# Output projection with its sums and lo parts on VectorE, and a ConvFFN entry that runs three first products in a row with lo parts from adding transfers

## The chip, the core and the metric

The kernel runs on one core of a Trainium2 chip. Its engines work in parallel, each on its own queue in order: TensorE (PE), VectorE (DVE), ScalarE (ACT), GpSimd (POOL) and SyncE (SP), which here only issues transfers. The metric is the device time of one execution in microseconds, from the first to the last instruction with what lies around it; smaller is better.

## The reference

One decoder layer over 1024 positions of width 1024 in float32: three token mixers on the same normalised input, merged by sigmoid gates, one output projection to the residual stream, and a gated MLP with a causal convolution of width 3 (ConvFFN, inner width 2816). The part that the change touches:

```python
merged = (gates[:, :, 0] * (y_sb @ w_sb_out[l])
          + gates[:, :, 1] * (y_ml @ w_ml_out[l])
          + gates[:, :, 2] * (y_xa @ w_xa_out[l]))
x = x + merged @ w_o[l]

h = _rmsnorm(x, g_ffn[l])
u = _causal_dwconv(h @ w_up[l], ff_conv_w[l], ff_conv_b[l])
u_val, u_gate = jnp.split(u, 2, axis=-1)
x = x + (jax.nn.silu(u_gate) * u_val) @ w_down[l]
```

## The kernel before

**Products.** A float32 operand is split into a hi part (a copy by ACT, rounded to the format that PE takes) and a lo part (operand minus hi, by VectorE), by `split` (L128). A product of two split operands is three matmuls of 128x128 by 128x512 (`mm3`, L142 to L144: hi by hi, hi by lo, lo by hi). Large products are cut into 2x2 blocks and done with seven block products instead of eight, from sums and differences of blocks (Strassen-Winograd). `au`, `al`, `bu`, `bl` are the blocks of the moving operand, `t1` to `t4` their sums; `a1`, `b1`, `a2`, `b2` are the blocks of a weight, `s1`, `s2` and the differences their sums. Tiles come from pools by tag, each with a fixed number of buffers that are given out in turn; a new tile waits until its buffer's last user is done. The stages that matter follow each other so:

**Branch products** (L1117 on). Three branches `b` of eight iterations. Each iteration makes one block of 128 output channels for both halves of the positions: for each half 12 matmuls into one of two banks `ps_pj`, and VectorE evicts it with the gate (L1137 for the first branch; L1139, then the addition L1140, for the others). Every other iteration loads a weight `raw` that is split into `whi` and `wlo`, two buffers each. Gates come from DRAM into five `U` buffers. Beside the iterations of branches 1 and 2 runs `beside`, the generators `wo_sums(0)` and `wo_sums(1)`: they load eight pages of the output projection's weights (tag `pg`, L1071, into pages that branch 0 has given back), make four sums for each half on POOL, and for each sum call `spill` (L1076): ACT copies the hi part to a `y` tile, POOL subtracts it into another `y` tile (two buffers in all), and POOL stores this lo part to `slo_d` in DRAM.

**Output projection** (stages 1 to 7, `stage`, 48 matmuls each). Stages 1, 2 and 5 take weights as loaded; 3, 4, 6 and 7 take the sums by `sum_w` (L1173): ACT copies hi again, POOL loads lo from `slo_d`. In stage 7 VectorE also scales the upper half's four `full` pages by the row factors and splits them into `dau` and `dbu`, the operands `au` and `bu` of the ConvFFN.

**ConvFFN entry.** Each of 22 units is a generator `seven`, advanced by `next`; a unit's products are, in order, first (`a1` by `au`), second (`b1` by `bu`), t2 and t3, t1, and `bl` and t4. A weight half is split by `qring` into a pair of tiles from a ring of four (`whi` and `wlo`, two buffers each). The lower half's row factors are not known at the start: `rstd` sums the squares over the partitions on PE (L158), VectorE scales the sums, POOL takes the root (L150), `spread` makes a diagonal on VectorE (L166) and spreads it over the partitions on PE. Then VectorE makes `diff`, `full` and from them t2, t3, t1, `bl` and t4, in this order, with their splits. In the program order the first unit's first product stands ahead of `rstd`, its second between `rstd` and `spread`, and the first and second products of the next two units behind.

Instructions are listed in program order, and a list scheduler may pull them forward; `tc.high_priority(offset=n)` moves the instructions in it n places ahead.

Of the kernel before, what the change touches and what calls it, by code (L numbers as in the profile page):

```python
# [10 lines left out]
F32 = mybir.dt.float32  # L11
# [7 lines left out]
P = 128  # L19
D = 1024  # L20
S = 1024
# [21 lines left out]
def tile_hybrid_layer(ctx: ExitStack, tc: tile.TileContext, xT, memT, vecs, w_t, w_n, w_kv, w_if,  # L43
# [55 lines left out]
    def dtile(shape, name):  # L99
        return dr.tile(shape, F32, tag=name, name=name)  # L100
# [22 lines left out]
        return vec[:, i:i + n]  # L123


    SOON = 40

    def split(src, hi, lo, eng=None):  # L128
        nc.scalar.activation(hi, src, AF.Copy)  # L129
# [531 lines left out]

    def qring(src, soon=SOON):
        t = pair(turn(0, ("whi", "wlo")))
        with tc.high_priority(offset=soon):
            split(src, *t)
        return t

    def prod(p, a, b, start=True):
        for k in range(4):
            mm3(p, a[0][:, ts(k)], a[1][:, ts(k)], *b[k], start and k == 0, k == 3, not start)  # L670
# [16 lines left out]
        nc.vector.tensor_sub(a2, a1, a2)  # L687
        nc.vector.tensor_sub(s2, s1, a1)

    def seven(w1, w2, x, done, ready=None):  # L690

        w, s1, s2, hl1 = ready or ((*halves(w1, next(RAWS[0])), *halves(w2, next(RAWS[1]))), None, None, None)
        a1, b1, a2, b2 = w
        L, p2 = bank(turn(2, LONG)), bank(turn(3, SHORT))
        prod(L, hl1 or qring(a1), x["au"])
        c1 = wide()
        up, lo = c1[:, hs(1)], c1[:, hs(0)]
        nc.scalar.activation(up, L, AF.Copy)
        if ready:
            yield  # L700
        prod(p2, qring(b1), x["bu"])
        nc.vector.tensor_add(up, up, p2)
        if not ready:
            s1, s2 = half(), a1
            sums(w, s1, s2)
        yield
        prod(L, qring(s2, 1000 if ready else SOON), x["t2"], False)
        c2 = wide()
        nc.scalar.activation(c2[:, hs(1)], L, AF.Copy)
        R = bank(turn(3, SHORT))  # L710
        prod(R, qring(a2, 1000 if ready else SOON), x["t3"])
        yield
        prod(L, qring(s1), x["t1"], False)
        nc.scalar.activation(c2[:, hs(0)], L, AF.Copy)
        nc.vector.tensor_add(c2[:, hs(0)], c2[:, hs(0)], R)
        nc.vector.tensor_sub(b1, b1, s2)
        yield
        prod(L, qring(b1), x["bl"], False)
        nc.scalar.activation(lo, L, AF.Copy)
        done(0, c1)  # L720
        prod(R, qring(b2), x["t4"], False)
        nc.vector.tensor_add(c2[:, hs(1)], c2[:, hs(1)], R)  # L722
        done(1, c2)
        yield
# [326 lines left out]
    slo_d = dtile([4, 2, P, S], "slo_d")  # L1051

    def block(n, h):
        return merged[n // 4][h][n % 4 // 2][:, hs(n % 2)]
# [18 lines left out]

    ws = [[None, None] for _ in range(4)]

    def spill(i, j):  # L1076
        hi, lo = T([P, S], "y", F32R), T([P, S], "y")
        nc.scalar.activation(hi, ws[i][j], AF.Copy)
        nc.gpsimd.tensor_sub(lo, ws[i][j], hi.bitcast(F32))
        nc.gpsimd.dma_start(slo_d[i, j], lo)  # L1080

    def wo_sums(j):
        a1, a2 = wo_load(0, 0, j, "pg"), wo_load(0, 1, j, "pg")
        yield
        nc.gpsimd.tensor_sub(a2, a1, a2)
        ws[2][j] = a2
        spill(2, j)
        b2 = wo_load(1, 1, j, "pg")
        yield
        nc.gpsimd.tensor_sub(b2, b2, a2)  # L1090
        ws[1][j] = b2
        spill(1, j)
        b1 = wo_load(1, 0, j, "pg")
        yield
        nc.gpsimd.tensor_add(a1, a1, b2)
        ws[0][j] = a1
        spill(0, j)
        nc.gpsimd.tensor_sub(b1, b1, b2)
        ws[3][j] = b1
        spill(3, j)  # L1100
        yield

    def fine(src, *tags):
        t = [T([P, S], tag, F32R) for tag in (tags[0], tags[-1])]
# [11 lines left out]
    ths = {i: get_gate(i, "y") for i in range(2)}  # L1116
    ys = None  # L1117
    w1 = []
    beside = itertools.chain(wo_sums(0), wo_sums(1))
    for i in range(3 * KT):  # L1120
        b, n = i // KT, ORDER[i % KT]
        if n == 0:
# [48 lines left out]
        return wsplit(None, raw=wo_load(q, i, j, "raw"))  # L1171

    def sum_w(i, j):  # L1173
        t = [T([P, S], tag, F32R) for tag in ("whi", "wlo")]
        nc.scalar.activation(t[0], ws[i][j], AF.Copy)
        nc.gpsimd.dma_start(t[1], slo_d[i, j])
        return t

    def out_tiles(i, h, tag):
        t = [T([P, S], tag) for _ in range(2)]  # L1180
# [147 lines left out]
    def ffn_up(f):  # L1328
        ys = {}

        def done(g, c):
            i = g * NF + f
            ys[g] = y = T([P, S], "y")
            conv(c, [col(C_FW + 3 * i + 2 - s) for s in range(3)], col(C_FB + i), y)
            if g:
                nc.scalar.activation(y, y, AF.Silu)
                nc.vector.tensor_mul(ys[0], ys[0], y)
                if f // 2 == 5:
                    nc.sync.dma_start(act_d[5, f % 2], ys[0])
# [4 lines left out]
        return seven(w_up[f], w_up[NF + f], fx, done, early if f == 0 else None)  # L1344


    fd, fx = {}, {"au": bau, "bu": bbu}
# [276 lines left out]
```

## Time and profile before

| | us |
|---|---|
| median of three runs | 1661.03 |
| lowest and highest | 1660.67, 1663.19 |
| the profiled execution, its own time | 1663.59 |
| its span | 1661.8 |
| mean granted PE clock | 0.994 |

A row of the timeline gives start and duration in us, engine, line, operation, output and inputs, shape, count, and in brackets the idle time of the engine ahead of it with what ended it. A row of waits gives the waiting instruction, what it waited for, the total, the number of waits and the longest. DVE is VectorE, ACT ScalarE, POOL GpSimd, SPq SyncE's queue. Matmuls overlap, so their durations exceed the distance of their starts.

### The profile page before, as it was taken

Reading aid. Unit: us, or ns where it says so; the run is one execution under the profiler, and the core shown is the slowest. Engines: PE = TensorE matmul, PEld = TensorE weight load, DVE = VectorE, ACT = ScalarE, POOL = GpSimd, SP = SyncE. Lnnn points to the kernel's source line nnn. Section 1 sums busy time; section 2 is a strip of 40 time slices with the busy share of each in tenths; the row PEclk is TensorE's granted clock in tenths of the full one; section 3 lists DMA queues with packets and bytes.
Section 4 is the critical chain, followed back from the end, with each engine's and each line's share of the span. In section 5 each row is a group of like instructions: output and inputs, shape, how many; then the busy total and the mean of one; then the engine's idle time right before and its main releaser. Section 6 shows DMA issues by size and latency. Waiting matters only on the chain.

```text
span 1661.8 us, 21230 instructions
## 1 busy us (share of the span) xinstructions
PE 1621.1 (98%) x7959; PEld 1325.5 (80%) x7959; DVE 1227.1 (74%) x1669; ACT 837.7 (50%) x1278; POOL 144.4 (9%) x196
## 2 busy tenths in 40 slices
PE   8999999999999999999977999999999999999999
PEld 4878888888788888888766887788888888888887
DVE  5658888859665676766565878997778877789864
ACT  4557777546554445666311355555555544543431
POOL 1022222020000101000072000000000000000000
PEclk9999999999999999999989999999999999999999
DMA  8420011424325564336865344132222221487131
GB/s 295 153 65 27 32 39 64 161 88 149 124 96 170 184 190 158 122 127 203 284 234 199 121 157 151 57 114 89 76 77 76 89 101 52 170 311 241 40 135 72
DMA packets 102515, 220.05 MB, mean 132 GB/s; under 512 B 13384, under 2 KB 37256, under 8 KB 102412
## 3 DMA queue, kind: packets, MB, share of 16 engines
q1 hardware_dynamic: 100108, 210.30, 37.4%
q0 software_dynamic: 2304, 8.39, 1.6%
q8 instruction: 63, 1.03, 0.3%
q14 instruction: 40, 0.33, 0.1%
HBM read 159.86 MB, written 58.80 MB: 132 GB/s over the span
## 4 chain that ended last, share of the span: by engine, by line
PE 86%; DMA 5%; DVE 3%; issue 3%; POOL 2%; ACT 2%; SPq 0%; POOLq 0%; DVEq 0%; ACTq 0%
PE ps_pj L142 12%; PE ps_pj L143 12%; PE ps_pj L144 12%; PE ps_pv L142 5%; PE ps_pv L144 5%; PE ps_pv L143 5%; PE ps_tr L142 4%; PE ps_tr L144 4%; PE ps_tr L143 4%; PE ps_z L142 4%; PE ps_z L143 4%; PE ps_z L144 4%; PE ps_pv L440 2%; PE ps_tr L420 2%; DMA raw<-in_w_kv_dram 1%
## 5 line engine op out<-in xcount | busy, mean ns | idle before, releaser
L143 PE MATMUL ps_pj<-h,whi 128*128 128x512 f32 x520 | 205.5, 395 | 1.3 <-DVE h L130 1.3
L142 PE MATMUL ps_pj<-h,whi 128*128 128x512 f32 x440 | 178.2, 405 | 19.9 <-DVE U L1139 18.1
L129 ACT ACTIVATE whi<-raw 128x512 fp32r<-128x512 f32 (+1 forms) x101 | 82.5, 816 | 139.9 <-PE ps_pj L143 43.8
L144 PE MATMUL ps_pj<-h,wlo 128*128 128x512 f32 x352 | 139.5, 396 | 0.1
L831 DVE SCALAR_TENSOR_TENSOR y<-U,vec,y 128x1023 f32<-128x1023 f32 x88 | 112.6, 1280 | 8.2 <-ACT y L829 8.1
L143 PEld LDWEIGHTS ps_pj<-h,whi 128*128 128x128 f32 x520 | 99.3, 191 | 21.1 <-DVE h L130 1.6
L142 PEld LDWEIGHTS ps_pj<-h,whi 128*128 128x128 f32 x440 | 84.1, 191 | 38.3 <-DVE U L1139 19.4
L408 DVE TENSOR_TENSOR_SCAN U<-U 128x512 f32<-128x512 f32 (+3 forms) x96 | 92.9, 1009 | 21.9 <-POOL U L403 20.3
L142 PE MATMUL ps_pj<-pg,whi 128*128 128x512 f32 x268 | 105.2, 393 | 1.2 <-DVE pg L1137 1.2
L144 PE MATMUL ps_pj<-pg,wlo 128*128 128x512 f32 x248 | 96.8, 390 | 0.0
L130 DVE TENSOR_TENSOR wlo<-raw,whi 128x1024 fp32r<-128x1024 f32 x44 | 54.4, 1237 | 39.8 <-ACT whi L129 39.7
L144 PEld LDWEIGHTS ps_pj<-h,wlo 128*128 128x128 f32 x352 | 67.4, 192 | 15.2 <-DVE wlo L130 0.6
L143 PE MATMUL ps_pv<-h,whi 128*128 128x512 f32 x190 | 74.1, 390 | 0.0
L143 PE MATMUL ps_pj<-pg,whi 128*128 128x512 f32 x188 | 73.5, 391 | 0.0
L129 ACT ACTIVATE whi<-pg 128x512 fp32r<-128x512 f32 (+1 forms) x46 | 35.3, 768 | 62.7 <-PE ps_z L143 18.2
L829 ACT ACTIVATE y<-U,vec 128x1024 f32<-128x1024 f32 x44 | 54.6, 1241 | 17.2 <-DVE U L722 17.2
L144 PE MATMUL ps_pj<-h,whi 128*128 128x512 f32 x160 | 62.4, 390 | 0.0
L142 PEld LDWEIGHTS ps_pj<-pg,whi 128*128 128x128 f32 x268 | 50.4, 188 | 13.0 <-DVE pg L1137 2.7
L142 PE MATMUL ps_pv<-h,whi 128*128 128x512 f32 x150 | 59.0, 393 | 0.4 <-DVE U L722 0.4
L144 PE MATMUL ps_pv<-h,wlo 128*128 128x512 f32 x152 | 59.2, 390 | 0.0
L130 DVE TENSOR_TENSOR wlo<-raw,wlo 128x512 fp32r<-128x512 f32 x55 | 37.8, 688 | 26.2 <-ACT wlo L129 26.0
L397 ACT ACTIVATE U<-ps_z 128x1024 f32<-128x1024 f32 (+3 forms) x48 | 39.1, 814 | 31.9 <-PE ps_z L395 24.1
(484 smaller groups left out, 4543.5 us busy)
## 6 DMA issues: line engine op xcount, KB each, us to landing
raw<-in_w_t_dram SPq DMA_DIRECT2D x29, 512.0 KB
gate_d<-U SPq DMA_DIRECT2D x24, 512.0 KB
U<-gate_d SPq DMA_DIRECT2D x22, 512.0 KB
act_d<-y SPq DMA_DIRECT2D x22, 512.0 KB
pg<-in_w_t_dram SPq DMA_DIRECT2D x21, 512.0 KB
raw<-in_w_dn_dram SPq DMA_DIRECT2D x18, 512.0 KB
h<-act_d SPq DMA_DIRECT2D x14, 512.0 KB
raw<-in_w_br_dram SPq DMA_DIRECT2D x12, 512.0 KB
```

The costliest lines, as they stand in the source:

```text
L129: nc.scalar.activation(hi, src, AF.Copy)
L130: (eng or nc.vector).tensor_sub(lo, src, hi.bitcast(F32))
L142: nc.tensor.matmul(out, lh, rh, start=start, stop=False, skip_group_check=more)
L143: nc.tensor.matmul(out, lh, rl, start=False, stop=False, skip_group_check=more)
L144: return nc.tensor.matmul(out, ll, rh, start=False, stop=stop, skip_group_check=more)
L397: nc.scalar.activation(f[:, :, 1:w + 1], z[:, :, :w], AF.Sigmoid, scale=-0.125)
L408: nc.vector.tensor_tensor_scan(f[:, a, 1:w + 1], f[:, a, 1:w + 1], f[:, a, 1:w + 1], 1.0 if o == 0 else f[:, a, 0:1], op0=ALU.mult, op1=AL ...
L420: nc.tensor.transpose(pt[:, a, ts(j)], g[:, a, ts(j)], ident)
L440: nc.tensor.matmul(pv[64 * a:64 * a + 64, ts(rb % 4)], sbv[s // 2][:, s % 2, (2 * p + a) * 64:(2 * p + a + 1) * 64], wt[a][:, ts(j)], star ...
L829: nc.scalar.activation(out, u, AF.Identity, bias=bias, scale=taps[0])
L831: nc.vector.scalar_tensor_tensor(out[:, :S - s], u[:, s:], taps[s], out[:, :S - s], op0=ALU.mult, op1=ALU.add)
```

## The change

Four things change.

- `wo_sums` is one generator. It loads the eight pages over four iterations, and the eight sums are made in place by VectorE, one per iteration in program order. `spill` and the DRAM tensor `slo_d` are gone.
- `sum_w` splits a sum with `fine`: hi by ACT as before, lo by VectorE at the time of use. POOL has no part in the output projection's weights any more.
- `seven` gets `pause` (units 0 to 2): a break after the first product. The entry then runs the first products of units 0, 1 and 2, and behind them their second products; `rstd` stands behind the first of them and `spread` behind the second.
- `seven` gets `adds` (units 0 to 3): the lo parts of `a1`, `b1` and `b2`, which are weights as they stand in DRAM, are made by `qadd`: ACT copies hi, ACT copies minus hi into the lo tile, and a transfer by POOL adds the weight from DRAM to it (256 KB, 11 of them in all, since the first unit's `a1` keeps its early split). `LEAD` (60) takes the place of `SOON` (40) as their priority.

```diff
-    SOON = 40
+    SOON, LEAD = 40, 60
...
+    def qadd(src, dram, soon=SOON):
+        t = pair(turn(0, ("whi", "wlo")))
+        with tc.high_priority(offset=soon):
+            nc.scalar.activation(t[0], src, AF.Copy)
+            nc.scalar.activation(t[1], t[0].bitcast(F32), AF.Copy, scale=-1.0)
+            nc.gpsimd.dma_start(t[1], dram, accum_op=ALU.add)
+        return t
...
-    def seven(w1, w2, x, done, ready=None):
+    def seven(w1, w2, x, done, ready=None, adds=False, pause=False):
+
+        def raw(src, w, i):
+            return qadd(src, w[:, hs(i)], LEAD) if adds else qring(src)
...
-        prod(L, hl1 or qring(a1), x["au"])
+        prod(L, hl1 or raw(a1, w1, 0), x["au"])
...
-        if ready:
+        if pause:
             yield
-        prod(p2, qring(b1), x["bu"])
+        prod(p2, raw(b1, w1, 1), x["bu"])
...
-        prod(R, qring(b2), x["t4"], False)
+        prod(R, raw(b2, w2, 1), x["t4"], False)
...
-    def spill(i, j):
-        hi, lo = T([P, S], "y", F32R), T([P, S], "y")
-        nc.scalar.activation(hi, ws[i][j], AF.Copy)
-        nc.gpsimd.tensor_sub(lo, ws[i][j], hi.bitcast(F32))
-        nc.gpsimd.dma_start(slo_d[i, j], lo)
...
-    def wo_sums(j):
-        a1, a2 = wo_load(0, 0, j, "pg"), wo_load(0, 1, j, "pg")
-        yield
-        nc.gpsimd.tensor_sub(a2, a1, a2)
-        ws[2][j] = a2
-        spill(2, j)
...
+    def wo_sums():
+        raw = []
+        for j in range(2):
+            for qi in (((0, 0), (0, 1)), ((1, 1), (1, 0))):
+                raw += [wo_load(q, i, j, "pg") for q, i in qi]
+                yield
+        for j in range(2):
+            a1, a2, b2, b1 = raw[4 * j:4 * j + 4]
+            for i, op, out, x, y in ((2, nc.vector.tensor_sub, a2, a1, a2), (1, nc.vector.tensor_sub, b2, b2, a2),
+                                     (0, nc.vector.tensor_add, a1, a1, b2), (3, nc.vector.tensor_sub, b1, b1, b2)):
+                op(out, x, y)
+                ws[i][j] = out
+                yield
...
     def sum_w(i, j):
-        t = [T([P, S], tag, F32R) for tag in ("whi", "wlo")]
-        nc.scalar.activation(t[0], ws[i][j], AF.Copy)
-        nc.gpsimd.dma_start(t[1], slo_d[i, j])
-        return t
+        return fine(ws[i][j], "whi", "wlo")
...
     next(first[0])
     r = rstd(acc[0], HALF)
-    next(first[0])
+    next(first[1])
     rows = spread(r, 4)
-    for u in first[1:]:
+    next(first[2])
+    for u in first:
         next(u)
```

Lines behind `qring` move, so the eviction L1139 and its addition L1140 are L1136 and L1137 in the new kernel, the split L130 stays, and a sum is L1096.

ScalarE's queue in the branch products of before, from the second branch's second weight on (`whi` is a branch weight's hi part, `y` the hi part of a sum that `spill` makes):

```order
L129 ACTIVATE whi_7486<-raw_7484 128x1024
L1078 ACTIVATE y_7477<-pg_7442 128x1024
L1078 ACTIVATE y_7523<-pg_7482 128x1024
L129 ACTIVATE whi_7576<-raw_7574 128x1024
L1078 ACTIVATE y_7563<-pg_7440 128x1024
L1078 ACTIVATE y_7569<-pg_7528 128x1024
L129 ACTIVATE whi_7658<-raw_7656 128x1024
```

and the same place after the change:

```order
L129 ACTIVATE whi_7481<-raw_7479 128x1024
L129 ACTIVATE whi_7559<-raw_7557 128x1024
L129 ACTIVATE whi_7631<-raw_7629 128x1024
L129 ACTIVATE whi_7727<-raw_7725 128x1024
L129 ACTIVATE whi_7799<-raw_7797 128x1024
```

The eight copies to `y` have left the queue, and the weights' hi parts stand next to each other.

VectorE's queue at the start of the second branch before, evictions from `ps_pj` with their additions:

```order
L1139 SCALAR_TENSOR_TENSOR U_7346<-U_7346,ps_pj_7408 128x512
L1140 TENSOR_TENSOR pg_7079<-pg_7079,U_7346 128x512
L1139 SCALAR_TENSOR_TENSOR U_7346<-U_7346,ps_pj_7423 128x512
L1140 TENSOR_TENSOR pg_7077<-pg_7077,U_7346 128x512
L1139 SCALAR_TENSOR_TENSOR U_7376<-U_7376,ps_pj_7444 128x512
```

and after, where L1096 is a sum of two loaded pages:

```order
L1136 SCALAR_TENSOR_TENSOR U_7345<-U_7345,ps_pj_7407 128x512
L1137 TENSOR_TENSOR pg_7079<-pg_7079,U_7345 128x512
L1096 TENSOR_TENSOR pg_7441<-pg_7439,pg_7441 128x1024
L1096 TENSOR_TENSOR pg_7475<-pg_7475,pg_7441 128x1024
L1136 SCALAR_TENSOR_TENSOR U_7345<-U_7345,ps_pj_7422 128x512
L1096 TENSOR_TENSOR pg_7439<-pg_7439,pg_7475 128x1024
L1137 TENSOR_TENSOR pg_7077<-pg_7077,U_7345 128x512
L1136 SCALAR_TENSOR_TENSOR U_7375<-U_7375,ps_pj_7443 128x512
L1096 TENSOR_TENSOR pg_7477<-pg_7477,pg_7475 128x1024
```

The scheduler has pulled the first four sums from iterations 12 to 15 into iterations 8 and 9; the second half's four stand in iterations 10 and 11.

VectorE's queue in the ConvFFN entry before, from the last scaled `full` page to the first use of the spread row factors (`whi`, `wlo` with L130 are lo parts of the weights, `h` with L130 of `dbu`):

```order
L1210 TENSOR_TENSOR pg_8246<-pg_8246,hf_8609 128x1024
L130 TENSOR_TENSOR whi_8778<-raw_8772,whi_8778 128x512
L130 TENSOR_TENSOR wlo_8795<-raw_8772,wlo_8795 128x512
L130 TENSOR_TENSOR h_8524<-pg_8246,h_8523 128x1024
L148 TENSOR_SCALAR sm_8745<-ps_tr_8740 128x4
L130 TENSOR_TENSOR whi_8821<-raw_8815,whi_8821 128x512
L166 TENSOR_SCALAR hf_8765<-ident,sm_8747 128x128 x4
L702 TENSOR_TENSOR U_8738<-U_8738,ps_pv_8725 128x512
L130 TENSOR_TENSOR wlo_8838<-raw_8815,wlo_8838 128x512
L1210 TENSOR_TENSOR h_8515<-h_8515,ps_tr_8770 128x1024
```

and after:

```order
L1204 TENSOR_TENSOR pg_8205<-pg_8205,hf_8568 128x1024
L130 TENSOR_TENSOR h_8481<-pg_8204,h_8480 128x1024
L148 TENSOR_SCALAR sm_8704<-ps_tr_8699 128x4
L130 TENSOR_TENSOR h_8483<-pg_8205,h_8482 128x1024
L166 TENSOR_SCALAR hf_8732<-ident,sm_8706 128x128 x4
L727 TENSOR_TENSOR me_8457<-me_8457,U_8463 128x512
L130 TENSOR_TENSOR whi_8834<-U_8463,whi_8834 128x512
L1204 TENSOR_TENSOR h_8474<-h_8474,ps_tr_8737 128x1024
```

The weights' lo parts have left this stretch (one more stood just ahead of it); a subtraction of unit 0's later weights (L727) and the split of its `s2` have moved into it, and the addition of its second product (L702 before, L713 now) has moved out, behind the splits of t2 and t3.

More of the change, by code (lines that the diff above doesn't have):

```diff
@@ L1050, in tile_hybrid_layer @@
     merged = [[[page() for _ in range(2)] for _ in range(2)] for _ in range(2)]
-    slo_d = dtile([4, 2, P, S], "slo_d")
     def block(n, h):
@@ L1074, in tile_hybrid_layer @@
     ws = [[None, None] for _ in range(4)]
-    def spill(i, j):
-        hi, lo = T([P, S], "y", F32R), T([P, S], "y")
-        nc.scalar.activation(hi, ws[i][j], AF.Copy)
-        nc.gpsimd.tensor_sub(lo, ws[i][j], hi.bitcast(F32))
-        nc.gpsimd.dma_start(slo_d[i, j], lo)
-    def wo_sums(j):
-        a1, a2 = wo_load(0, 0, j, "pg"), wo_load(0, 1, j, "pg")
-        yield
-        nc.gpsimd.tensor_sub(a2, a1, a2)
-        ws[2][j] = a2
-        spill(2, j)
[L1088 to L1101, printed above, removed]
+    def wo_sums():
[11 more added lines that the diff above has]
+                yield
     def fine(src, *tags):
@@ L1118, in tile_hybrid_layer @@
     w1 = []
-    beside = itertools.chain(wo_sums(0), wo_sums(1))
+    beside = wo_sums()
     for i in range(3 * KT):
@@ L1342, in done @@
                                       ys[0].rearrange("p (h r) -> p h r", h=2))
-        return seven(w_up[f], w_up[NF + f], fx, done, early if f == 0 else None)
+        return seven(w_up[f], w_up[NF + f], fx, done, early if f == 0 else None, f < 4, f < 3)
     fd, fx = {}, {"au": bau, "bu": bbu}
```

## The prediction

> **What bounds the kernel now.** The busy shares come first, then the windows of the stage that the change rewrites, then who waited for whom there.
>
> ```profile
> PE 1621.1 (98%) x7959; PEld 1325.5 (80%) x7959; DVE 1227.1 (74%) x1669; ACT 837.7 (50%) x1278; POOL 144.4 (9%) x196
> 820.00:840.00 20.00, 20.00 (x89) 16.35 (x88) 14.20 (x15) 4.00 (x4) 4.91 (x2) 1.00 0.94 326
> 840.00:860.00 20.00, 17.73 (x72) 14.12 (x70) 12.15 (x12) 3.07 (x3) 15.93 (x9) 0.91 0.80 277
> 860.00:880.00 20.00, 12.57 (x46) 9.89 (x45) 9.57 (x9) 3.06 (x3) 15.02 (x8) 0.74 0.40 130
> 880.00:900.00 20.00, 11.56 (x44) 9.11 (x43) 9.71 (x11) 5.18 (x5) 9.44 (x8) 0.83 0.38 138
> 900.00:920.00 20.00, 20.00 (x90) 16.58 (x89) 12.86 (x18) 3.19 (x3) 0.00 (x0) 1.00 0.67 233
> ```
>
> Each window row gives its length, then the busy time of PE, PEld, DVE, ACT and POOL, the granted clock, the DMA share and GB/s. PE is busy 98% of the span, so only its holes can be won. The largest lies in 840 to 900: 162 matmuls where 270 fit at the 90 per 20 us of the next row. It begins when POOL begins and ends with it.
>
> ```profile
> ACT y L1078 <- POOL y L1079: 43.8, 7, 10.6
> DVE wlo L130 <- ACT whi L129: 21.7, 4, 10.6
> PE ps_pj L142 <- DVE U L1139: 18.1, 3, 8.4
> POOL y L1079 <- DMA slo_d<-y: 16.7, 5, 4.7
> ```
>
> These rows (wait, total us, times, longest) are one chain. `spill` has two `y` buffers per tag and gives each back only when its store has landed; ACT stands before the next `y`, with the branch weights' `whi` behind it; VectorE stands before `whi`, with the eviction L1139 behind it; PE stands before the bank.
>
> The size of the hole comes from those evictions, two per branch iteration:
>
> ```profile
> 831.72 0.69 DVE L1139 SCALAR_TENSOR_TENSOR U<-U,ps_pj 128x512 f32<-128x512 f32 x1 [0.62 <-PE ps_pj L144]
> 834.44 0.69 DVE L1139 SCALAR_TENSOR_TENSOR U<-U,ps_pj 128x512 f32<-128x512 f32 x1 [1.31 <-PE ps_pj L144]
> 902.55 0.69 DVE L1139 SCALAR_TENSOR_TENSOR U<-U,ps_pj 128x512 f32<-128x512 f32 x1 [1.30 <-PE ps_pj L144]
> 831.00:903.00 72.00, 12.05 (x18) 0.86 0.60 208
> ```
>
> The first two and the last wait for PE, 2.72 us apart (12 matmuls of 0.227). The last row counts 18 of them, 17 steps: 46.2 us at PE's pace, 70.8 in the trace. The hole is **24.6 us**: 18.1 of waiting and 6.5 mostly of matmuls at a granted clock below 1.
>
> The second hole is the entry to the ConvFFN:
>
> ```profile
> 1020.00:1040.00 20.00, 18.01 (x78) 13.41 (x77) 19.05 (x27) 9.67 (x13) 1.40 (x1) 1.00 0.16 54
> 1040.00:1060.00 20.00, 16.15 (x69) 12.44 (x68) 20.00 (x26) 9.21 (x14) 0.00 (x0) 1.00 0.08 22
> 1053.68 0.51 PE L142 MATMUL ps_pj<-h,whi 128*128 128x512 f32 x1 [1.74 <-ACT h L129]
> 1055.47 0.50 PE L143 MATMUL ps_pj<-h,whi 128*128 128x512 f32 x1 [1.28 <-DVE h L130]
> ```
>
> VectorE is full there and PE is not: the operand of t1 comes last, after everything queued ahead of it on VectorE.
>
> **Branch stage.** The 16 POOL subtractions, eight ACT copies, eight stores and the `y` buffers behind the chain go, so the whole 24.6 us can go. What is late next is VectorE, which gets eight sums and has to wait for their data.
>
> ```profile
> 835.01 2.40 POOL L1085 TENSOR_TENSOR pg<-pg,pg 128x1024 f32<-128x1024 f32 x1 [77.34 <-DMA pg<-in_w_o_dram]
> 826.83 1.45 SPq L1071 DMA_DIRECT2D pg<-in_w_o_dram  x3
> 832.45 0.69 DVE L1140 TENSOR_TENSOR pg<-pg,U 128x512 f32<-128x512 f32 x1
> 944.42 1.22 DVE L1113 TENSOR_TENSOR pg<-pg,pg 128x1024 f32<-128x1024 f32 x1
> 945.56 1.22 DVE L130 TENSOR_TENSOR h<-pg,h 128x1024 fp32r<-128x1024 f32 x1
> ```
>
> A 128x1024 operation occupies VectorE for 1.14 us (the last two starts), an eviction and its addition 0.72 each. POOL's first sum started when its two loads had landed, at 835.0. Those loads go out behind as many transfers as before, so I keep that time. The new order puts two sums between iteration 8's two evictions: the first 835.0 to 836.2; the second needs the third load, by the 1.6 us that a 512 KB transfer takes at 326 GB/s at about 836.5, so it ends at 837.6. The eviction due at 834.4 ends at 838.3. PE has two banks, fills the next until 837.2, and loses **1.1 us**. From there, four further groups hold 4 x 1.44 of evictions, 4 x 1.14 of sums and a weight split of 1.14 (11.5 us) against 10.9 of PE: 0.2 us more by my step-by-step count. Bounds for the sums: 0, and all eight in the open, 9.1 us. I take **1.3**, since evictions have a bank of slack.
>
> Does a wait of 1.1 us cost clock as well?
>
> ```profile
> 805.00:810.00 5.00, 3.78 (x17) 2.79 (x17) 2.96 (x4) 3.07 (x3) 0.00 (x0) 1.00 0.30 87
> 847.56 0.50 PE L142 MATMUL ps_pj<-h,whi 128*128 128x512 f32 x1 [2.27 <-DVE U L1139]
> 850.00:855.00 5.00, 5.00 (x19) 3.94 (x18) 2.41 (x5) 0.00 (x0) 2.22 (x1) 0.77 0.77 292
> ```
>
> A hole of 1.2 us left the clock at 1.00; after one of 2.27 us, 850 to 855 ran at 0.77. So 1.1 us costs none, and a wait above 2 us some 1.7 us on top (about 3.4 us at half pace). The Trainium skill (TensorE: Matmul & The Clock Gate, HAM oscillation) warns only of idle gaps longer than about 3.4 us; the trace disagrees, since 2.27 us was followed by 0.77. By the Trainium skill's rule a late load of 4 us still costs clock, and one below 3.4 us its wait alone: 1.7 us less than the trace says.
>
> **Output projection.** Eight lo parts, loaded before, become VectorE splits.
>
> ```profile
> 940.00:960.00 20.00, 20.00 (x90) 16.59 (x89) 19.73 (x23) 12.16 (x14) 0.54 (x1) 1.00 0.42 125
> 960.00:980.00 20.00, 20.00 (x90) 16.58 (x89) 15.13 (x19) 11.43 (x14) 1.62 (x3) 1.00 0.44 139
> 956.72 1.07 ACT L1175 ACTIVATE whi<-pg 128x1024 fp32r<-128x1024 f32 x1 [2.43 <-PE ps_pj L143]
> 957.22 0.54 POOL L1176 DMA_DIRECT2D wlo<-slo_d  x1 [58.18 <-PE ps_pj L144]
> DMA to landing us min/median/max: 2.9/4.2/6.9
> ```
>
> PE has no hole here. The first hi part ends at 957.8; today's lo part lands about 4.2 after 957.2, at 961.4. A split ends at 958.9, earlier. The first two splits fall where VectorE is fullest and push evictions by 1.1 us, against a bank that is needed a stage half (5.4 us) later. **0**, cover: VectorE's idle time from 960 on (4.9 us in that row alone). Without cover 8 x 1.14 = 9.1 us; the gain side is 0, as PE never waited here.
>
> **Entry.** PE now does three first products (8.2 us) before it needs an operand of the second kind, so its small waits at 1023 to 1030 go; but t1 sets the end, so VectorE is counted up to it.
>
> ```profile
> 1022.10 1.02 PE L158 MATMUL ps_tr<-ones,hf 128*128 128x1 f32 x8 [0.27 <-DVE hf L1206]
> 1021.87 0.69 DVE L130 TENSOR_TENSOR wlo<-me,wlo 128x512 fp32r<-128x512 f32 x1
> 1022.47 0.75 DVE L1313 SCALAR_TENSOR_TENSOR h<-y,sm,pg 128x512 f32<-128x512 f32 x1
> 1029.44 0.87 DVE L166 TENSOR_SCALAR hf<-ident,sm 128x128 f32<-128x128 f32 x4 [0.93 <-POOL sm L150]
> 1031.54 1.22 DVE L1210 TENSOR_TENSOR h<-h,ps_tr 128x1024 f32<-128x1024 f32 x1
> 1054.19 1.22 DVE L130 TENSOR_TENSOR h<-y,h 128x1024 fp32r<-128x1024 f32 x1
> ```
>
> VectorE pauses once in the 40 us of the two windows, 0.93 us for a root on POOL. Five splits of 0.60 (1021.87 to 1022.47) go, and the root comes earlier: 3.9 us at most. But the product that spreads the row factors now stands on PE behind three first products. The first ends at about 1021.4 (the row sums of L158 follow it after two matmuls and 0.27 us); then come 5 matmuls, the row sums (1.0), 19 and 2 matmuls and the spreading product, which I put at the same 1.0: 1029.3. So the multiplication that starts at 1031.54 now starts at about 1029.4. From there to t1 the queue is as long as before (one split leaves it, an addition joins; one subtraction leaves, another split joins). **2.1 us** gained, bounds 0 and 3.9. PE still waits about 3 us for t1, which hides up to 3 us of lateness in the five transfers before it.
>
> **The adding transfers.** Eleven lo parts become two ACT copies and a POOL transfer of 256 KB that adds in flight. No row shows one; nearest is the 512 KB load:
>
> ```profile
> wlo<-slo_d POOLq DMA_DIRECT2D x8, 512.0 KB, 4.4
> 1012.92 0.63 ACT L129 ACTIVATE whi<-raw 128x512 fp32r<-128x512 f32 x1 [1.05 <-DMA x_d<-px]
> 1018.36 0.63 ACT L129 ACTIVATE whi<-raw 128x512 fp32r<-128x512 f32 x1 [1.07 <-PE ps_z L143]
> ```
>
> I take its 4.4 us to landing, between the row's 2.9 and twice 4.4, if reading the destination doubles the work. Entry: the first two copies start at 1012.9, their negated copies end near 1014.6 and 1015.7, they land near 1019.1 and 1020.2, and the third matmuls need them from 1021.7 and 1024: covered. The next two, from 1018.4, land near 1025.9, needed from 1029. Units 0 to 3, after the entry: a pair comes free, ACT copies twice (0.63 each, plus up to 2 us behind its queue), POOL issues 0.54, the transfer takes 4.4: 6 to 8 us, while the ring of four pairs gives three products, 8.2, minus what is interleaved. I count one overhang of 0.4 and one of 0.5: **0.9 us**, bounds 0 and, at 8.8, 6.2. VectorE is relieved of six more splits there; PE, at its matmuls' pace from 1056 on, gains nothing by it. By the Trainium skill (DMA: Bandwidth & Descriptors, Anatomy of one DMA) a POOL transfer takes 2.0 us plus its bytes at 436 GB/s: an estimate of 2.6 us for 256 KB, and these 0.9 us would be nothing. It gives 3.2 for 512 KB, where the rows show 4.4, so the measured one stands.
>
> **Sum.** -24.6 + 1.3 + 0 - 2.1 + 0.9 = -24.5 us. The profiled execution took 1663.59 us (span 1661.8), the median of the three runs is 1661.03, and they reach 1663.19; a stall of engines should repeat in all of them, so I subtract from the median: **1636.5 us**.
>
> **Rivals.**
> - Transfers at twice the row, 8.8 us: 6.2 instead of 0.9, 1641.8. For it: an add reads its destination too. Against: half the bytes. 0.13. The Trainium skill (DMA: Bandwidth & Descriptors, Rules for kernel authors) says that an accumulating transfer reads its destination and writes it later, which is this mechanism; no row here shows one.
> - The sums' loads land 4 us later, behind the residual loads that the new order moves up: 4 us of wait and 1.7 of clock, 1642.2. Against: as many transfers stand ahead as before. 0.13.
> - VectorE becomes the bound and all 16 operations are in the open: 18.2 minus the counted 1.3, 1653.4. Against: its idle time in the windows. 0.04.
> - The stall is not POOL's alone, and the DMA queues hold PE for half of the hole: 1648.8. Against: shares 0.40 and 0.38 inside it. 0.02.
> - **Slower:** the adding transfers take so long that the ring starves PE. Beyond 8.8 us each us costs some 4 us (entry once, three pairs behind one another), so 19.2 us are eaten at about 13.6 us to landing; at 15.5 the time is about 1669. Against: the longest POOL transfer took 6.9 us with the DMA at 0.9. 0.04.
>
> Forecast 0.64. The range takes the hole closed without loss and 3.9 in the entry, 1632.5, up to late loads (5.7), late transfers (5.3) and 1.5 us of uncovered sums together, 1649. Faster by over 0.2% (3.3 us, about what a measurement of this kernel can tell): 0.94; within: 0.02; slower: 0.04.
>
> **What would show it.** PE busy 20.00 and clock 1.00 in the 20 us windows after iteration 9; one wait of about 1 us on L1136 near 837; no wait of ACT on POOL; no hole in the output projection; the wait for t1 still about 3 us but 2 us earlier relative to the first product; adding transfers landing in 3 to 5 us. Wrong would be a wait on a POOL transfer in PE's rows, or an eviction behind a sum for more than 2 us.

## The result and the profile after

| | before | after |
|---|---|---|
| median, us | 1660.85 (1657.98 to 1663.19, 4 runs) | 1638.81 (1638.00 to 1639.59, 4 runs) |
| profiled execution: span, us | 1661.8 | 1637.9 |
| mean granted PE clock | 0.994 | 0.998 |

The ratio is 0.9868, with a 95% interval of 0.9851 to 0.9885. The predicted 1636.5 us is 2.3 us below the median; the medians differ by 22.0 us and the spans by 23.9, since the profiled execution of before took 1663.59 us, above all its timed runs.

From the page of after, the engines' busy time:

```profile
PE 1617.3 (99%) x7959; PEld 1322.9 (81%) x7959; DVE 1225.8 (75%) x1674; ACT 835.1 (51%) x1281; POOL 104.4 (6%) x175
```

The windows of after over the branch stage (columns as in the prediction):

```profile
820.00:840.00 20.00, 18.69 (x81) 14.85 (x80) 13.33 (x17) 3.09 (x4) 0.00 (x0) 1.00 0.92 316
840.00:860.00 20.00, 20.00 (x90) 16.56 (x89) 17.37 (x24) 2.11 (x2) 0.00 (x0) 1.00 0.77 277
860.00:880.00 20.00, 20.00 (x90) 16.57 (x89) 12.60 (x17) 2.13 (x2) 0.00 (x0) 1.00 0.43 143
880.00:900.00 20.00, 20.00 (x90) 16.57 (x89) 14.53 (x19) 3.18 (x3) 0.00 (x0) 1.00 0.44 145
```

From 840 on PE is full at clock 1.00 where before had 17.73, 12.57 and 11.56, and POOL's busy time is 0. All waits of PE between 780 and 1070 in after:

```profile
PE ps_pj L142 <- ACT h L129: 2.7, 1, 2.7
PE ps_pj L142 <- DVE U L1136: 1.3, 1, 1.3
PE ps_pj L142 <- DVE pg L1134: 1.3, 1, 1.3
PE ps_tr L142 <- ACT whi L129: 0.4, 1, 0.4
PE ps_pv L142 <- ACT wlo L129: 0.4, 1, 0.4
```

The wait on L1134, an eviction of the first branch, came at 818.95; before has one like it on its L1137 (1.22 us at 808.91). The one on L1136 is new, and the one on `h` is the wait for t1. The timeline of after around the new wait, rows of VectorE and one of PE (837.16):

```profile
831.11 0.68 DVE L1136 SCALAR_TENSOR_TENSOR U<-U,ps_pj 128x512 f32<-128x512 f32 x1
...
833.94 2.57 DVE L1096 TENSOR_TENSOR pg<-pg,pg 128x1024 f32<-128x1024 f32 x2 [1.42 <-DMA pg<-in_w_o_dram]
836.42 0.68 DVE L1136 SCALAR_TENSOR_TENSOR U<-U,ps_pj 128x512 f32<-128x512 f32 x1
...
837.16 0.50 PE L142 MATMUL ps_pj<-h,whi 128*128 128x512 f32 x1 [1.31 <-DVE U L1136]
...
878.29 0.69 DVE L1136 SCALAR_TENSOR_TENSOR U<-U,ps_pj 128x512 f32<-128x512 f32 x1 [1.31 <-PE ps_pj L144]
```

Two sums stand ahead of an eviction and wait for a load; PE stands behind it for 1.31 us. The eviction began some 2.6 us after its matmuls allowed it: the last of them started at 832.74, and in before an eviction that waits for PE starts 1.1 us behind that. The 18th eviction begins at 878.29: the 17 steps that took 70.8 us in before take 47.2.

A second reading splits each span in three at the first and the last of the stage's 32 evictions (16 branch iterations, two each): the time up to the first, the stage, and the rest with the output projection, the entry and all of the ConvFFN behind it. The experiments below stand in the same table, which is put together from their timelines; medians are of the timed runs, and each ratio is to runs of before taken beside that kernel.

| kernel | median us | ratio to before (95%) | span | first eviction | stage | rest |
|---|---|---|---|---|---|---|
| before | 1660.85 | | 1661.8 | 831.72 | 109.10 | 720.98 |
| after | 1638.81 | 0.9868 (0.9851 to 0.9885) | 1637.9 | 831.11 | 85.45 | 721.34 |
| e11_after_again | 1638.59 | 0.9853 (0.9834 to 0.9872) | 1637.6 | 830.52 | 85.19 | 721.89 |
| e1_proj_only | 1643.16 | 0.9877 (0.9859 to 0.9894) | 1639.6 | 831.30 | 85.22 | 723.08 |
| e2_entry_only | 1662.62 | 0.9998 (0.9986 to 1.0011) | 1661.9 | 831.96 | 108.07 | 721.87 |
| e3_gpsimd_sums | 1643.50 | 0.9878 (0.9862 to 0.9894) | 1641.5 | 830.52 | 89.62 | 721.36 |
| e4_no_store | 1663.61 | 1.0002 (0.9992 to 1.0012) | 1659.1 | 828.29 | 110.21 | 720.60 |
| e9_no_copy | 1646.61 | 0.9908 (0.9890 to 0.9926) | 1644.0 | 828.69 | 94.63 | 720.68 |
| e13_copy_on_gpsimd | 1658.66 | 0.9975 (0.9962 to 0.9989) | 1657.1 | 829.40 | 104.82 | 722.88 |
| e5_no_adds | 1642.28 | 0.9883 (0.9867 to 0.9900) | 1641.1 | 832.72 | 85.79 | 722.59 |
| e6_old_order | 1645.08 | 0.9894 (0.9873 to 0.9916) | 1644.0 | 831.70 | 86.02 | 726.28 |
| e8_t1_first | 1637.85 | 0.9857 (0.9840 to 0.9874) | 1634.9 | 829.44 | 85.08 | 720.38 |
| e12_t1_first_again | 1638.16 | 0.9851 (0.9833 to 0.9868) | 1636.4 | 831.42 | 85.17 | 719.81 |

Between before and after the stage gives 23.65 us, the way to it 0.6, and the rest takes 0.4 back. The first eviction comes between 828.29 and 832.72 in these profiles although nothing ahead of it was changed (PE's first matmul starts between 6.2 and 7.6 us, and its waits on evictions between 780 and 828 sum to between 0 and 1.6), so a span by itself can mislead by 4 us. The stage is surer: in the seven profiles that share after's stage (after, e11, e1, e5, e6, e8, e12) it ranges over 0.9 us. The rest ranges over 1.3 in the five that share all of it (after, e11, e3, e4, e9), so smaller differences of the rest tell nothing by themselves.

In the entry PE gets its t1 operand earlier, and then runs slowly. PE's rows of after:

```profile
1024.84 0.39 PE L144 MATMUL ps_pv<-pg,wlo 128*128 128x512 f32 x1
1027.92 0.79 PE L142 MATMUL ps_pj<-h,whi 128*128 128x512 f32 x1 [2.69 <-ACT h L129]
...
1029.18 0.79 PE L143 MATMUL ps_pj<-h,whi 128*128 128x512 f32 x1
1029.77 0.63 PE L144 MATMUL ps_pj<-h,whi 128*128 128x512 f32 x1
...
1034.46 0.40 PE L144 MATMUL ps_tr<-h,wlo 128*128 128x512 f32 x1
```

The first L143 matmul of t1 is the first that needs VectorE's lo part. It stands 114.65 us behind the last eviction in before (1055.47 from 940.82) and 112.62 in after (1029.18 from 916.56): 2.0 us gained. The multiplication by the spread row factors, from which the prediction counted t1, moved as it had said: 90.72 us behind the last eviction in before (1031.54), 88.57 in after (1005.13). From 1029.77 to 1034.46 are 11 steps (from one matmul's start to the next), 4.69 us instead of 2.50 at the 0.227 of before: 2.2 us lost again. The window shows the clock:

```profile
1020.00:1040.00 20.00, 17.27 (x61) 12.98 (x62) 18.18 (x21) 10.35 (x15) 0.86 (x1) 0.83 0.19 52
```

Before, its window 1040 to 1060 stood at 1.00 after waits of 1.74 and 1.28 us.

Last, the groups of adding transfers of after (KB each, median us to landing):

```profile
wlo<-in_w_up_dram POOLq DMA_DIRECT2D x6, 256.0 KB, 6.1
whi<-in_w_up_dram POOLq DMA_DIRECT2D x5, 256.0 KB, 6.6
```

### The profile page after: what moved, and what is told of

It reads as the page before. It is cut to its first block, busy times and chain, and to the rows that moved or that the text cites. A ratio compares the mean times of both kernels' runs of the same rounds, so it can differ in the third digit from the quotient of the medians.

```text
span 1637.9 us, 21193 instructions
## 1 busy us (share of the span) xinstructions
PE 1617.3 (99%) x7959; PEld 1322.9 (81%) x7959; DVE 1225.8 (75%) x1674; ACT 835.1 (51%) x1281; POOL 104.4 (6%) x175
## 4 chain that ended last, share of the span: by engine, by line
PE 93%; DMA 2%; DVE 2%; ACT 2%; issue 1%; POOL 0%; SPq 0%; DVEq 0%; ACTq 0%; POOLq 0%
PE ps_pj L142 13%; PE ps_pj L144 13%; PE ps_pj L143 13%; PE ps_pv L144 6%; PE ps_pv L142 6%; PE ps_pv L143 6%; PE ps_tr L142 4%; PE ps_tr L143 4%; PE ps_tr L144 4%; PE ps_z L142 4%; PE ps_z L144 4%; PE ps_z L143 4%; PE ps_pv L440 2%; PE ps_tr L420 2%; PE ps_z L395 1%; PE ps_z L394 1%
## 5 line engine op out<-in xcount | busy, mean ns | idle before, releaser
L143 PE MATMUL ps_pj<-h,whi 128*128 128x512 f32 x520 | 204.1, 393 | 0.0
L143 PEld LDWEIGHTS ps_pj<-h,whi 128*128 128x128 f32 x520 | 98.3, 189 | 20.0 <-DVE h L130 0.8
L129 ACT ACTIVATE whi<-pg 128x512 fp32r<-128x512 f32 (+1 forms) x53 | 43.1, 815 | 66.2 <-PE ps_tr L143 18.3
L143 PE MATMUL ps_pv<-h,whi 128*128 128x512 f32 x190 | 74.0, 389 | 0.0
L143 PE MATMUL ps_pj<-pg,whi 128*128 128x512 f32 x188 | 73.4, 390 | 0.0
L130 DVE TENSOR_TENSOR wlo<-raw,whi 128x1024 fp32r<-128x1024 f32 x44 | 53.7, 1221 | 17.3 <-ACT whi L129 17.3
L130 DVE TENSOR_TENSOR wlo<-raw,wlo 128x512 fp32r<-128x512 f32 x53 | 36.5, 688 | 26.6 <-ACT wlo L129 26.3
L144 PE MATMUL ps_tr<-pg,wlo 128*128 128x512 f32 x144 | 56.0, 389 | 0.0
```

The source lines that it names most:

```text
L130: (eng or nc.vector).tensor_sub(lo, src, hi.bitcast(F32))
L143: nc.tensor.matmul(out, lh, rl, start=False, stop=False, skip_group_check=more)
L144: return nc.tensor.matmul(out, ll, rh, start=False, stop=stop, skip_group_check=more)
```

## The experiments

**Which half of the change gives the time.** Two kernels take the change apart: in the first the units get `adds=False`, only unit 0 pauses, and the first products stand in the old order; the second keeps `spill`, `slo_d` and the old `sum_w` with the new entry.

```diff
-        return seven(w_up[f], w_up[NF + f], fx, done, early if f == 0 else None, f < 4, f < 3)
+        return seven(w_up[f], w_up[NF + f], fx, done, early if f == 0 else None, False, f == 0)
...
-    next(first[1])
+    next(first[0])
     rows = spread(r, 4)
-    next(first[2])
-    for u in first:
+    for u in first[1:]:
         next(u)
```

> The new output projection with the old ConvFFN entry. Theory (the trace of after): all of the gain that is left at the end comes from the branch stage, where the 17 eviction steps went from 70.8 to 47.2 us, and the entry's 2.7 us were lost again to TensorE at half pace after its 2.69 us wait. Then this kernel takes about as long as after, 1638 to 1640 us, with a span near 1638, and its t1 waits are a pair like before's 1.74 + 1.28 us with full pace behind them. Rival A (the entry's gain is lasting, as the prediction had it, 1.2 us net): 1640 to 1641.5. Rival B (the entry gives most of the 24 us by starting the ConvFFN earlier): 1650 or more.

> The old output projection (GpSimd's sums, the two y buffers, the stores to slo_d) with the new ConvFFN entry. Theory: the hole of the branch stage is there again, steps of 70 us for 17 evictions, and the entry is worth 0 to 2.7 us according to whether TensorE runs at half pace behind the t1 wait: 1658 to 1661 us. Rival (the entry carries much of the gain): below 1652.

The stage takes 85.22 us in e1 and 108.07 in e2: the projection closes the hole alone, and the entry alone is level with before. By the median e1 is above what was expected; by its ratio it cannot be told from after. What e1 adds is the clock. The timeline of PE in e1, at before's own pair of waits:

```profile
1029.38 0.50 PE L142 MATMUL ps_pj<-h,whi 128*128 128x512 f32 x1 [1.75 <-ACT h L129]
1031.16 0.80 PE L143 MATMUL ps_pj<-h,whi 128*128 128x512 f32 x1 [1.28 <-DVE h L130]
1031.76 0.63 PE L144 MATMUL ps_pj<-h,whi 128*128 128x512 f32 x1
```

The waits are before's to 0.01 us, and so is the distance from the last eviction (1031.16 - 916.52 = 114.64). But here half pace follows, against the expectation, and the rest is 723.08 instead of 720.98: **2.1 us**, all of it behind this L143 (608.44 instead of 606.33 us to the span's end), where PE's 2651 matmuls stand in the same order. So after's entry has to be compared with e1's: its rest is 1.7 and 1.2 us shorter (721.34 and 721.89), about the spread given above, so that this gain is likely and its size is not shown. Before's profile is the exception: of the eleven profiles in which PE waits 1.7 us or more for t1 (all but e8, e12), only that one shows no half pace behind.

**What makes the hole.** e3 keeps the sums on GpSimd without `spill`. e4 keeps `spill` with ACT's copies and GpSimd's subtractions, without the store. e9, one step on, takes ACT's copies away. In all three the lo parts that the products use come from VectorE, as in after. Against e2:

```diff
 e4 and e9:
-        nc.gpsimd.dma_start(slo_d[i, j], lo)
...
 e9:
-        hi, lo = T([P, S], "y", F32R), T([P, S], "y")
+        lo = T([P, S], "y")
-        nc.scalar.activation(hi, ws[i][j], AF.Copy)
-        nc.gpsimd.tensor_sub(lo, ws[i][j], hi.bitcast(F32))
+        nc.gpsimd.tensor_sub(lo, ws[i][j], ws[i][j])
```

> After, but the eight sums of the output projection stay on GpSimd at the places that they had before; no hi and lo are made there, nothing is stored, and the lo parts come from VectorE as in after. Theory (the hole is the chain of two y buffers, the store and the activation queue behind it, not GpSimd's sums): the hole stays closed but for VectorE's adds beside GpSimd, which took 2.15 to 2.80 us instead of 0.69 before; evictions that shared the time with GpSimd stood 2.80 us apart instead of 2.72, so eight sums of 2.4 to 2.9 us (some 20 us) cost below 2 us: 1638 to 1641 us. Rival (GpSimd's adds slow VectorE and with it the evictions; that is the hole): half of the hole or more is back, 1650 us or more.

> Before's projection with its GpSimd sums, the activation copies into y and GpSimd's subtractions of the lo parts, but the lo parts are not stored to slo_d and not read back (the lo parts used come from VectorE); the new entry. Theory: of the chain the landing of the stores is gone (GpSimd waited 3.63 + 4.66 + 2.50 + 2.50 + 3.42 = 16.7 us for them); the sixteen GpSimd operations follow each other for some 40 us, and a weight split behind a y copy waits for one or two of them, so most of the hole is closed: 1640 to 1647 us. Rival A (GpSimd's time itself is the hole): 1655 to 1661 us. Rival B (the stores alone made it all): 1638 to 1639.5 us.

> As e4_no_store, with its sixteen GpSimd operations at the same places, but the activation engine's eight copies into y are gone: each lo subtraction takes the sum from itself, a result that nothing reads (the product's lo parts come from VectorE). It tells the two halves of what e4 left: the activation queue, in which the weight split's copy stood behind y copies that wait for GpSimd (at 872.37 us behind eight of them), or GpSimd's operations beside VectorE's. Theory Q (the queue): PE's waits on the evictions fall from e4's 21.8 us to what GpSimd costs beside VectorE; e3's eight sums in 22.5 us cost 3.3 us of waits, so sixteen cost 6 to 8 us: span 1643 to 1647 us. Rival P (GpSimd's operations beside VectorE are the hole): span 1656 to 1661 us as in e4.

e3's stage is 89.62 us: the eight sums on GpSimd cost 4.2, more than expected, because VectorE's splits of 128x1024 beside them took 3.4 us (1.22 alone), not only the additions 2.2. PE's one long wait there, 3.10 us, stands behind the split shown, and half pace follows it for 8 steps. Timeline of e3, VectorE:

```profile
852.04 2.18 DVE L1148 TENSOR_TENSOR pg<-pg,U 128x512 f32<-128x512 f32 x1
854.15 3.38 DVE L130 TENSOR_TENSOR wlo<-raw,whi 128x1024 fp32r<-128x1024 f32 x1
```

e4 is a miss: without any store the hole is whole, 110.21 us. ACT's rows of e4 show why:

```profile
871.41 1.06 ACT L1089 ACTIVATE y<-pg 128x1024 fp32r<-128x1024 f32 x1 [3.55 <-POOL y L1090]
872.37 1.04 ACT L129 ACTIVATE whi<-raw 128x1024 fp32r<-128x1024 f32 x1
```

The `y` copies follow GpSimd's pace, about 5.3 us each (839.56 to 871.41 in six steps), and the second weight split's `whi` stands behind all eight of them. Without the stores the scheduler also put more copies ahead of it (in before two, two and three stand between the splits), so e4 does not weigh the stores' landing at before's order. e9 decides what it was made for: GpSimd's sixteen operations run over nearly the same stretch (832.82 to 874.35 us, in e4 831.52 to 874.89), ACT's queue is clear, and the stage is 94.63 us. PE's waits on evictions, e4 first, then e9:

```profile
PE ps_pj L142 <- DVE U L1149: 21.8, 2, 15.0
```

```profile
PE ps_pj L142 <- DVE U L1148: 7.3, 4, 2.3
```

Of e4's 24.8 us over after, clearing the activation queue gives back **15.6** (110.21 - 94.63), and **9.2** remain (94.63 - 85.45). Three of e9's four waits, 5.8 us, stand behind VectorE's operations beside GpSimd; the eight sums alone cost 4.2 (e3). The fourth, 1.46 us at 884.72, comes when GpSimd is done: the eviction waits for a branch weight whose load stood in SyncE's queue behind residual loads into `y` tiles, which GpSimd's subtractions held. SyncE's wait in e9 (us in total, times, longest):

```profile
SPq L1189 <- POOL y L1089: 24.7, 2, 19.5
```

The stores' share was tried from the other side: with the stores kept, GpSimd makes the `y` copies itself.

```diff
-        nc.scalar.activation(hi, ws[i][j], AF.Copy)
+        nc.gpsimd.tensor_copy(hi, ws[i][j])
```

> As e2_entry_only (GpSimd's sums, two y buffers, stores to slo_d, lo parts read back), but the eight copies into y are made by GpSimd instead of the activation engine, so the landing of the stores and the y buffers still hold GpSimd, and nothing that waits for them stands ahead of the weight splits' copies. It tells what e4 left open, whether the stores' landing matters by itself. Measured so far from the first to the last of the 32 evictions: 108.1 us in e2, 110.2 in e4, 94.6 in e9, 85.5 in after. Theory Q (only what stands in the activation queue ahead of the weight split stalls PE; beside it GpSimd's time slows VectorE, 9.2 us for sixteen operations): 24 operations cost at most 14 us, 92 to 100 us in this stage, span 1645 to 1653. Rival L (the landing of the stores holds PE by another way): 105 us or more, span above 1657.

The stage is 104.82 us, between the two expectations, and the rows fit neither. VectorE's and GpSimd's timelines of e13:

```profile
847.21 5.87 DVE L1151 TENSOR_TENSOR pg<-pg,U 128x512 f32<-128x512 f32 x1
853.00 0.68 DVE L1150 SCALAR_TENSOR_TENSOR U<-U,ps_pj 128x512 f32<-128x512 f32 x1
...
846.82 1.06 POOL L1089 CAST y<-pg 128x1024 fp32r<-128x1024 f32 x1
847.82 2.41 POOL L1109 TENSOR_TENSOR pg<-pg,pg 128x1024 f32<-128x1024 f32 x1
850.18 2.34 POOL L1090 TENSOR_TENSOR y<-pg,y 128x1024 f32<-128x1024 f32 x1
852.83 0.58 POOL L1091 DMA_DIRECT2D slo_d<-y  x1 [0.31 <-POOL y L1090]
```

An addition that takes 0.69 us alone began at 847.21 and ended at 853.08, when GpSimd had finished a copy, a sum and a subtraction and turned to issuing a transfer. Of PE's seven waits in this stage, 13.2 us, six (10.2) stand behind such stretched additions and splits. The seventh stands behind a branch weight that landed late near 911. SyncE's waits, its issue of that weight, and PE's wait:

```profile
SPq L1194 <- POOL y L1090: 15.6, 1, 15.6
SPq L1194 <- DMA slo_d<-y: 5.5, 1, 5.5
...
905.39 0.38 SPq L1137 DMA_DIRECT2D raw<-in_w_br_dram  x1
...
915.74 0.50 PE L142 MATMUL ps_pj<-h,whi 128*128 128x512 f32 x1 [3.00 <-DVE U L1150]
```

SyncE, too, works its queue in order: residual loads into `y` tiles stood for a subtraction and then 5.5 us for a store's landing, with the branch weight's load behind them. So a landing does reach PE by another way, as the rival had it, but for one wait of 3.00 us and the half pace behind it, out of the 19.4 us that the stage is longer than after's. The 8.7 us for which landings held GpSimd itself are not told apart from its operations here.

In before the landings stand on the chain as well: GpSimd waited 4.66 and 2.50 us for stores before the subtraction at 883.43, whose end let ACT make the copy at 885.79, and the weight split's `whi` at 886.75 stood behind that copy, ahead of PE's wait of 8.44 us. How much of before's hole the landings make stays open; that the queue behind them stalls PE without any store is shown by e4.

**The two halves of the entry.** e5 is after with `adds=False`; e6 is after with the old order (the lines of e1) and `pause` for unit 0 alone.

```diff
 e5:
-        return seven(w_up[f], w_up[NF + f], fx, done, early if f == 0 else None, f < 4, f < 3)
+        return seven(w_up[f], w_up[NF + f], fx, done, early if f == 0 else None, False, f < 3)
...
 e6:
-        return seven(w_up[f], w_up[NF + f], fx, done, early if f == 0 else None, f < 4, f < 3)
+        return seven(w_up[f], w_up[NF + f], fx, done, early if f == 0 else None, f < 4, f == 0)
...
```

> After without the adding transfers (VectorE makes these lo parts again), with the new order of the first products. Theory: the transfers save VectorE some five subtractions of 0.60 us ahead of t1, so t1 begins 2 to 3 us later relative to the entry's start, and half pace behind the wait comes in both: span 1640 to 1641. Rival 1 (the transfers' landing of 6.2 us and their issue cost as much as the subtractions that they save): span 1637 to 1638.5, as after. Rival 2 (the half pace falls elsewhere): below 1637.

> After with the adding transfers but with before's order of the first products (two products of the first unit ahead of the rows' spread). Theory: the root's pause of 0.93 us on VectorE's chain is there again, t1 begins 1 us later: span 1638.5 to 1639.5. Rival (the order brings nothing, since the t1 wait only takes it up): span 1637.5 to 1638.2.

With e1 and after these are the four corners. The rest is 723.08 with neither, 722.59 with the order alone, 726.28 with the transfers alone, and 721.34 and 721.89 with both. The distance from the last eviction to t1's first L143 tells them apart more sharply: 114.64 us with neither, 115.54 with the order alone, 117.90 with the transfers alone, and 112.62 and 112.40 with both. Neither half brings t1 forward by itself. e5 came as expected. e6 missed by 5 us, and its rows are those of the wait that the prediction named as what would make it wrong. GpSimd's issue and PE's wait in e6:

```profile
997.23 0.87 POOL L673 DMA_DIRECT2D whi<-in_w_up_dram  x1 [3.41 <-ACT whi L672]
...
1003.63 0.80 PE L144 MATMUL ps_pj<-pg,whi 128*128 128x512 f32 x1 [3.58 <-DMA whi<-in_w_up_dram]
1004.22 0.63 PE L142 MATMUL ps_pv<-h,wlo 128*128 128x512 f32 x1
```

6.4 us pass from the issue to the matmul. In the old order the third product comes too soon for that, and PE waits 3.58 us and falls to half pace; three first products in a row cover the transfer in after and e11. In e2 and e13, which have them too and in which GpSimd also loads the sums' lo parts, 1.35 and 0.87 us of wait on such a `whi` are left.

**Can t1's wait be had back?** e8 writes unit 2's sums behind the t1 products and gives t1's operands a priority.

```diff
+        if late:
+            sums(w, s1, s2)
...
+    with tc.high_priority(offset=30):
         for j in range(2):
             bl = x1p[2 + j]
```

> After, with the t1 operands brought forward on VectorE: the third unit's three sums (3 x 0.60 us) are written behind the first units' t1 products, and the t1 operands get a priority of 30. By the order and the durations of after's trace the first half of t1's operand ends near 1023.2 us, before TensorE is free at 1024.8, its 12 first-half matmuls last until 1027.5, the second half comes near 1028.5: one wait of about 1 us in place of after's 2.69. Theory (the entry's gain is lost in the t1 wait and in the half pace behind it, 11 steps of 0.43 us in place of 0.23): no half pace, 3.5 to 4.5 us faster than after, span 1633.5 to 1634.5. Rival (half pace comes whatever the wait, or the moved sums are late for the third unit): 0 to 2 us faster, span 1636 to 1638.

> The changed kernel itself once more, on the same chip and in the same rounds as the next kernel. Expected: 1638 to 1640 us, ratio to before 0.986 to 0.988, span near 1638 and half pace behind the t1 wait again, if the half pace is a fixed consequence of that wait; a span near 1635.5 without half pace, if it comes by chance.

> The kernel of e8_t1_first once more, beside the changed kernel. Theory (t1's wait and the half pace behind it are what the entry gave back): 2.5 to 3.5 us faster than e11_after_again in the medians and in the spans. Rival (e8's 3.0 us of span were chance): within 1 us of it.

The mechanism came: the wait is gone and no half pace follows. PE in e8:

```profile
1023.22 0.39 PE L142 MATMUL ps_pj<-h,whi 128*128 128x512 f32 x1
...
1027.08 0.50 PE L143 MATMUL ps_pj<-h,whi 128*128 128x512 f32 x1 [0.30 <-DVE h L130]
1027.42 0.39 PE L144 MATMUL ps_pj<-h,whi 128*128 128x512 f32 x1
```

The size did not. After's kernel once more, e11, shows the half pace again (9 steps, 1.6 us lost). The rest is 720.38 and 719.81 against 721.34 and 721.89, 1.5 us on average, since small waits take the place of the large one (0.9 on a `wlo`, 1.0 on a `whi`, 0.5 on an `h`); e4 and e9, with after's entry, have 720.60 and 720.68, so even this is hardly beyond chance. Of e8's 3.0 us in the span, 1.7 lay ahead of the stage. The medians of e12 and e11, on one chip in the same rounds, differ by 0.4 us, which the intervals do not resolve. So no better kernel is shown.

## Why the prediction was right, and where not

1. **The branch hole, -24.6.** Right in size: the stage gave 23.65 us net of the sums' 1.3, so 24.95 gross. The chain that it read from four wait rows is the one in before's rows: of PE's 18.1 us there, 15.9 stand behind weight splits that waited 9.44 and 10.55 us for `whi`. Its first link, a store that "must land", is not needed for a hole of this size: e4 has one without a store, at another order of the copies. What the chain leaves out is what GpSimd does beside the queue: with ACT's queue clear, e9 still loses 9.2 us, most of it to VectorE's operations stretched beside GpSimd's, which the rows of before show too (additions of 2.15 us instead of 0.69). A change that had cleared only the queue would not have had the whole 24.6.
2. **The eight sums, +1.3.** Right in mechanism, place and size: one wait of 1.31 us on L1136 at 837.16, no clock loss (820 to 840 at 1.00). The eviction's 2.6 us behind the sums is past the 2 us that the prediction named as a sign of being wrong; its own count had 3.2 (837.6 instead of 834.4), so that sign was set too low.
3. **The output projection, 0.** Right: no PE wait, 20.00 in each of its windows.
4. **The entry, -2.1.** The term itself was right, and by the mechanism named: the multiplication by the row factors came 2.15 us earlier and t1's L143 2.0. What was missing is a price. The prediction said that a wait above 2 us costs some 1.7 us of clock, and that t1's wait would stay at about 3 us, but it did not put the two together: the sum has no clock term behind t1's wait, and no reason is given. The rows that it shows have before's clock at 1.00 there, and that was this one execution: e1, with the same waits, lost 2.1 us. The step that failed is this term left at nothing; after lost 2.2 us there and e11 1.6. Nor is 1.7 us a fixed price of a wait above 2 us: behind one of 2.29 us in e9 (at 857.44) the pace is full.
5. **The adding transfers, +0.9.** The duration was too low: 6.1 and 6.6 us to landing instead of 4.4, and 0.86 us of issue instead of 0.54. Their price was of the right order and differs between executions. In after the rest lost 0.36 us while t1 gained 2.0 and the clock took 2.2, which leaves about 0.2 for them, and no wait of PE on one reached 0.5 us. In e11, the same kernel, the rest lost 0.91 while t1 gained 2.25 and the clock took 1.6, which leaves about 1.6, and PE waited 1.24 us for one behind the entry. That is the overhang that the prediction counted, and also the wait on a POOL transfer that it named as a sign of being wrong. Their relief of VectorE, in the entry's term, is real: without them t1's L143 comes 2.9 us later (e5). The Trainium skill (DMA: Bandwidth & Descriptors, Anatomy of one DMA) gave an estimate of 2.6 us for 256 KB; the trace disagrees with its 6.1.

The sum, -24.5 against -23.9 in the spans, holds one missing term and three small ones: the clock, +2.2; the transfers, -0.7; the hole, -0.35 more than counted; and the way to the first eviction, -0.6, which is chance. That the total is so near is partly luck, since the clock's term is set off by the others. By the medians, from which the forecast subtracts, the gain is 22.0, or 2.5 us less than forecast: the hole was read from an execution slower than all four timed runs of before in the table, and no second profile of before shows how long it is in the others (the same old projection in e2 has a stage of 108.07 instead of 109.10). Of the rivals none came. The measured 6.1 and 6.6 us of a transfer lie between the forecast's 4.4 and the rival's 8.8, and that rival's price did not come; its mechanism is what e6 shows.

## What to carry to other kernels

When a slow engine's results pass through a queue that also feeds the critical engine, look at what stands behind the waiting instruction there: taking the stores out left a hole of the same size (e4), taking the copies out of that queue as well gave back 16 us, and moving all of it to an engine with idle time 24. The queue that issues the loads can pass the wait on too (SyncE in e9 and e13). Price every wait of the bound engine with the clock that may fall behind it, and do not trust one execution in which it did not. An edit that loses alone (the transfers in e6) can gain beside another, so measure all four corners before dropping one.

## What was not expected of the hardware

- PE's clock can fall after a wait of less than 3 us: half pace for 11 steps (2.2 us) after a single wait of 2.69 us, and after a pair of 1.75 and 1.28. It does not always: the same pair in before and a wait of 2.29 us in e9 left full pace, so these runs give no threshold. The Trainium skill (TensorE: Matmul & The Clock Gate, HAM oscillation) names gaps of more than about 3.4 us; the traces disagree.
- VectorE's additions with two inputs in SBUF stretch beside GpSimd from 0.69 to 2.2 us, and in e13 to 5.87, over three GpSimd operations in a row. The Trainium skill (SBUF — State Buffer, SBUF: two separate sides) says that the one which comes first holds a shared port pair for its whole instruction; the trace agrees, and adds that VectorE can lose several rounds in succession. The evictions that read PSUM kept their 0.68.
- A transfer of 256 KB that adds takes longer to land (6.1 to 6.6 us) than a plain one of 512 KB on the same queue in before (4.4). What else moved at the time differs, so that the adding is the cause is not shown.
